# A two-layer attention trunk on one core: when the first rows are scaled, when two sets of weights are split, and which tiles the sine products use

## The chip, the cores and the metric

The kernel runs on one core of a Trainium2 chip. A core has five engines that work side by side, each on its own list of instructions: TensorE (PE, with its weight loads shown as PEld), VectorE (DVE), ScalarE (ACT), GpSimd (POOL) and SyncE (SP), which here only issues transfers (DMAs). An engine takes its instructions in order; where one waits, everything behind it on that engine waits too. The metric is the time of one execution in microseconds (us); the figure for a kernel is the median of its timed runs.

## The reference, cut to what matters

One sequence of 1024 tokens of width 1024 goes through two layers. All weights are float32. Before each of them the rows are normalised (RMS norm with a gain by column).

```python
def mla_swa_layer(x, ...):                         # layer 0
    z = rms_norm(x, g_in) @ w_in
    cq, ckv, kpe, q_s, k_s, v_s, gate = split_cols(z, EVEN_SPLITS)
    q  = rms_norm(cq, g_q_a) @ w_q_up              # 256 -> 8 heads of 64 + 32
    kv = rms_norm(ckv, g_kv_a) @ w_kv_up           # 128 -> 8 heads of 64 + 64
    # the 32 rotary columns of q and k are turned by the token's angle (cos, sin)
    o = concat(causal attention of q, kv; sliding window attention of q_s, k_s, v_s)
    return x + (o * silu(gate)) @ w_out
def fox_layer(x, ...):                             # layer 1
    q, k, v, f_logit, gate = split_cols(rms_norm(x, g_in) @ w_in, ODD_SPLITS)
    log_cum = cumsum(log_sigmoid(f_logit + b_f))   # bias log_cum[t] - log_cum[s] on the logits
    return x + (causal attention with that bias * silu(gate)) @ w_out
```

The output is the RMS norm of the last rows, times a gain.

## The kernel before, in words

**Number format.** Every operand of a product is held as two tiles, a high part (names with h: hh, wh, qh, kh) and the remainder (hl, wl, ql, kl). A product is three matmuls: L118 (high by high), L119, L120. The high part is a cast on ACT (L107 for rows, L112 and L792/L803 for weights), the low part is a subtraction: on DVE for rows (L108, which reads PSUM), on POOL for weights (L115, L805). A step of one input chunk or one weight tile is called its split.

**The start.** The token rows 0 to 511 lie in four tiles xrows[0..3] (called r in the profile), rows 512 to 1023 in xrows[4..7] (ld, kx). While they are loaded, PE runs 46 matmuls on zeros (L587, from tile ob). DVE and ACT sum the squares of rows 0 to 3 (L147, L150), DVE makes the inverse roots (`inv_rms`, twelve small instructions, L127 to L142). Then the rows are scaled, in two column halves (0 to 511, then 512 to 1023), each half in four instructions: row tile 0 on POOL (L287), row tile 1 on ACT (L795), row tiles 2 and 3 on DVE (L797). Between the halves a table of 19 gains is turned (PE L801) and copied (DVE L802, tile gains); every split of a chunk needs it. Behind them POOL makes the low parts of the four first weight tiles (L805) and a mask (L806).

**The first loop** (L812) goes over eight column chunks of 128, k = 0..7: PE turns the chunk's four 128x128 blocks (L216; here T0 to T7; T0 to T3 read the first column half, T4 to T7 the second), ACT makes hh (L107), DVE makes hl (L108), and one chunk later PE multiplies by the first weights (`latent_q`, L690, here L0 to L7: twelve matmuls each, first four with hh and the high weights, then four with hl, then four with the low weights). The turned blocks lie in PSUM tiles named s and t in turn, two of each. Between the chunks stand the sums of squares of rows 4 to 7 (k < 4), their `inv_rms` (k = 4) and scaling (k = 5, POOL L287 three times and DVE L824). For k > 5 two steps of `zb_steps` are taken in each turn: a step casts (ACT L112) and subtracts (POOL L115) one tile of the second weights, 288 columns wide, into kh and kl (six tiles) and kx (two tiles). These are used by `latent_kv`, eight chunks of three matmuls for each block of 128 tokens.

**Queries.** `up_q` (L914) multiplies the normalised latent by its weights; for the 32 rotary columns DVE multiplies the result by a table of cosines and by one of sines (L928), each into a tile of tag "r0", and SP stores the tile. Tag r0 has four buffers, tag "og" two.

**Values of layer 1.** Three groups of columns (256, 384, 384) are multiplied for all eight token blocks. `value_weights` loads and splits the weights of one group; those of group 2 (qh, ql, kh, kl) are asked for behind the last block of group 1. The forget logits come out of group 0; they are turned (PE L1281), summed along the sequence (lcs), stored and read back as the bias tiles ld.

**What sets the order.** In the start the code fixes the order of PE, DVE, ACT and POOL as it is written; later parts are put in order by a scheduler that follows the code's order and what is ready by its own estimate, so that moving a call moves its instructions on every engine.

Of the kernel before, what the change touches and what calls it, by code (L numbers as in the profile page):

```python
# [19 lines left out]
P = 128  # L20
S = 1024
D = 1024
NB = S // P
# [28 lines left out]
WORK0 = "q1 g0 q2 s0 q3 s1 s2 s3 a1 p0 b1 g2 p1 g3 p2"  # L52
WARM = 46
W_START0 = "FFFLLFLFLF"
# [7 lines left out]
def trunk(ctx, tc, x, positions, e_g_in, e_w_in, e_g_q_a, e_w_q_up, e_g_kv_a, e_w_kv_up,  # L62
          e_sinks, e_w_out, o_g_in, o_w_in, o_b_f, o_w_out, g_final, out):
    nc = tc.nc
    x, out = x[0], out[0]
# [29 lines left out]
    def pst(tag, n=512):  # L95
        count[0] += 1
        t = ps.tile([P, 512], F32, tag=tag, name=f"{tag}{count[0]}", bufs=BANKS[tag])
        return t[:, :n]
# [476 lines left out]
    gst = sbt("bs", [P])  # L575
# [9 lines left out]
    with tc.manual_schedule(engines={mybir.EngineType.PE}):  # L585
        for j in range(WARM):
            nc.tensor.matmul(out=idle, lhsT=zeros[:, 0:P], rhs=zeros[:, 0:512], start=True, stop=True)  # L587
# [188 lines left out]
    with tc.manual_schedule(engines={ET.PE, ET.DVE, ET.Activation, ET.Pool}):  # L776
# [8 lines left out]
        nc.vector.tensor_scalar(out=ssq[:, 3:4], in0=part[:, 0:1], scalar1=part[:, 1:2], scalar2=None, op0=ALU.add)  # L785
        y = inv_rms(ssq, 4, D)
        for k in range(0, KC, 4):
# [3 lines left out]
        for (wl, wh), raw in list(zip(za_low, za_raw))[:3]:  # L791
            nc.scalar.copy(out=wh, in_=raw)  # L792
        for c in (slice(0, 512), slice(512, D)):
            normalise(xrows[0][:, c], y[:, 0:1], 1.0)
            nc.scalar.activation(out=xrows[1][:, c], in_=xrows[1][:, c], func=AF.Copy, scale=y[:, 1:2])  # L795
            for b in (2, 3):
                nc.vector.tensor_scalar(out=xrows[b][:, c], in0=xrows[b][:, c], scalar1=y[:, b:b + 1],  # L797
                                        scalar2=None, op0=ALU.mult)
            if c.start == 0:
                g_ps = pst("pj", 32)  # L800
                nc.tensor.transpose(out=g_ps[:, 0:19], in_=gst[0:19], identity=ident[0:19, 0:19])  # L801
                nc.vector.tensor_copy(out=gains, in_=g_ps[:, 0:19])  # L802
        nc.scalar.copy(out=za_low[3][1], in_=za_raw[3])  # L803
# [7 lines left out]
        for k in range(KC + 2):  # L811
            made = next(turns, None) or made  # L812
            if k == 1:
                steps = latent_q(0)
            if k > 1:
                next(steps)
            if k < 4:
                square_sum(xrows[4 + k], ssq[:, k:k + 1], k == 1)
            if k == 4:
                y = inv_rms(ssq, 4, D)  # L820
            if k == 5:
                for b in range(3):
                    normalise(xrows[4 + b], y[:, b:b + 1], 1.0)
                nc.vector.tensor_scalar(out=xrows[7], in0=xrows[7], scalar1=y[:, 3:4], scalar2=None, op0=ALU.mult)  # L824
            if k > 5:
                for _ in range(2):
                    next(zb_steps, None)
# [86 lines left out]
    def up_q(g, i):  # L914

        for hf in range(2):
# [4 lines left out]
            if i < 2:  # L921
                st = sbt("r0", [512])
                nc.scalar.copy(out=st, in_=acc)
                nc.sync.dma_start(out=qns[2 * g + i, :, cols], in_=st)
            else:
                for table, to in ((cosT, qcs), (sinT, qss)):
                    st = sbt("r0", [512])
                    nc.vector.tensor_tensor(out=st, in0=acc, in1=table[:, cols], op=ALU.mult)  # L928
                    nc.sync.dma_start(out=to[g, :, cols], in_=st)
# [319 lines left out]
    for g in range(3):  # L1249
        c0, c1, parts, n = made  # L1250
        for blk in range(NB):
# [5 lines left out]
            if c0 == 0:  # L1257
                nc.vector.tensor_tensor(out=flog[:, blk, :], in0=acc[:, c1:n], in1=bf_b, op=ALU.add)
            if g < 2 and blk == (4 if g == 0 else NB - 1):
                made = value_weights(*groups[g + 1])  # L1260
# [195 lines left out]
```

## Time and profile before

| | us |
|---|---|
| timed runs | 1189.61, 1192.16, 1192.25 (median 1192.16) |
| the profiled execution | 1190.83 |
| its span, first to last instruction | 1189.0 |
| PE busy | 1161.2 (98%) |
| DVE, ACT, POOL busy | 716.0, 702.7, 588.8 (60%, 59%, 50%) |

The profiled execution is 1.8 us longer than its span and 1.3 us below the median. All positions below are us from the start of the span. In a row of the timeline the columns are start, duration, engine, line, operation, output tile <- input tiles, shape and count; in square brackets stands the idle time of the engine before it and what ended it. The matmuls overlap, so that the distance of two starts is what one costs.

### The profile page before, as it was taken

What the parts mean: (1) busy time and instruction counts of PE and PEld (TensorE: products, weight loads), DVE (VectorE), ACT (ScalarE), POOL (GpSimd) and SP (SyncE); (2) the same over time, 40 slices, a digit from 0 to 9 for tenths busy, and PEclk for the clock granted to TensorE, in tenths of its full rate; (3) what the DMA queues carried; (4) which work ended last, traced back from release to release, by engine and by line L of the source; (5) the groups of instructions that cost most, each with busy time, mean ns of one, the idle gap of its engine ahead of it and who ended that gap; (6) DMA issues with size and microseconds to landing.
All of it is one profiled execution on the core that took longest, in us unless ns stands there. A gap on an engine that the chain in (4) does not pass through costs nothing. (4 is left out here: it accounts for less than half of the span.)

```text
span 1189.0 us, 19541 instructions
## 1 busy us (share of the span) xinstructions
PE 1161.2 (98%) x6384; PEld 994.2 (84%) x6384; DVE 716.0 (60%) x1905; ACT 702.7 (59%) x1565; POOL 588.8 (50%) x717
## 2 busy tenths in 40 slices
PE   9999999999999999999999999999999999999997
PEld 6897788888888877899898888888888888887886
DVE  6672366687767766662103666665666666657754
ACT  6445567776666665554115766676767676766532
POOL 6411245474665453333404556656555555568452
PEclk9999999999999999999999999999999999999999
DMA  5327522453654442654322222313122223237441
GB/s 203 105 56 265 122 55 73 123 151 116 175 165 117 130 149 81 201 171 137 110 97 62 64 71 63 89 56 96 60 84 65 81 68 96 65 124 230 154 158 63
DMA packets 155357, 135.26 MB, mean 114 GB/s; under 512 B 53580, under 2 KB 119911, under 8 KB 155255
## 3 DMA queue, kind: packets, MB, share of 16 engines
q1 hardware_dynamic: 155254, 134.02, 38.1%
q8 instruction: 50, 0.82, 0.3%
q14 instruction: 53, 0.43, 0.1%
HBM read 96.43 MB, written 37.55 MB: 113 GB/s over the span
## 5 line engine op out<-in xcount | busy, mean ns | idle before, releaser
L118 PE MATMUL pj<-hh,wh 128*128 128x512 f32 (+1 forms) x792 | 320.4, 405 | 1.2 <-DVE ql L248 1.2
L120 PE MATMUL pj<-hh,wl 128*128 128x512 f32 (+1 forms) x792 | 308.9, 390 | 0.0
L119 PE MATMUL pj<-hl,wh 128*128 128x512 f32 (+1 forms) x792 | 308.8, 390 | 0.0
L115 POOL TENSOR_TENSOR wl<-wr,wh 128x512 fp32r<-128x512 f32 (+1 forms) x130 | 164.2, 1264 | 149.9 <-ACT wh L112 140.9
L105 DVE TENSOR_TENSOR pl<-t,ph 128x512 fp32r<-128x512 f32 (+1 forms) x320 | 179.0, 564 | 85.9 <-ACT ph L104 83.9
L287 POOL TENSOR_SCALAR r<-r,sm 128x256 f32<-128x256 f32 (+4 forms) x250 | 169.8, 688 | 123.1 <-DVE sm L334 66.6
L104 ACT CAST ph<-t 128x512 fp32r<-128x512 f32 (+1 forms) x320 | 153.9, 484 | 112.4 <-PE t L358 93.2
L120 PEld LDWEIGHTS pj<-hh,wl 128*128 128x128 f32 x792 | 148.8, 188 | 32.5
L332 ACT ACTIVATE r<-r,sm 128x128 f32<-128x128 f32 (+7 forms) x184 | 143.1, 778 | 54.1 <-DVE sm L325 52.5
L118 PEld LDWEIGHTS pj<-hh,wh 128*128 128x128 f32 x792 | 149.4, 189 | 22.8 <-issue 1.6
L119 PEld LDWEIGHTS pj<-hl,wh 128*128 128x128 f32 x792 | 149.7, 189 | 20.5
L358 PE MATMUL t<-ident,r 128*128 128x128 f32 x828 | 135.8, 273 | 7.9 <-DVE pl L105 5.1
L358 PEld LDWEIGHTS t<-ident,r 128*128 128x128 f32 x828 | 103.8, 140 | 35.8 <-DVE pl L105 6.3
L112 ACT CAST wh<-wr 128x512 fp32r<-128x512 f32 (+1 forms) x130 | 77.6, 598 | 60.0 <-PE pj L119 27.3
L319 POOL TENSOR_TENSOR ld<-ld,zrow 128x128 f32<-128x128 f32 x128 | 58.4, 465 | 105.8 <-DVE sm L325 79.2
L349 PE MATMUL o<-ph,v 128*128 128x512 f32 (+3 forms) x288 | 107.5, 373 | 0.0
L350 PE MATMUL o<-pl,v 128*128 128x512 f32 (+3 forms) x288 | 99.8, 347 | 0.0
L325 DVE CUSTOM_DVE_ANT_0 r<-s,ld 128x512 f32<-128x512 f32 (+1 forms) x120 | 67.6, 563 | 47.8 <-PE s L272 45.4
L296 POOL TENSOR_TENSOR v<-ge,v 128x512 fp32r<-128x512 f32 x26 | 33.8, 1300 | 68.7 <-ACT v L295 68.6
L349 PEld LDWEIGHTS o<-ph,v 128*128 128x128 f32 x288 | 54.7, 190 | 7.7
L350 PEld LDWEIGHTS o<-pl,v 128*128 128x128 f32 x288 | 54.9, 191 | 6.3
L248 DVE TENSOR_TENSOR qh<-pj,qh 64x512 fp32r<-64x512 f32 x24 | 16.4, 685 | 65.1 <-ACT qh L247 64.8
(335 smaller groups left out, 2355.6 us busy)
## 6 DMA issues: line engine op xcount, KB each, us to landing
wr<-in_o_w_in SPq DMA_DIRECT2D x50, 256.0 KB, 2.9
ld<-lcs SPq DMA_DIRECT2D x16, 512.0 KB, 4.3
ogs<-og SPq DMA_DIRECT2D x28, 256.0 KB, 2.0
wr<-ogs SPq DMA_DIRECT2D x28, 256.0 KB, 3.3
ge<-vscr SPq DMA_DIRECT2D x24, 256.0 KB, 3.9
gt<-x1s SPq DMA_DIRECT2D x23, 256.0 KB, 2.6
wr<-ogs SPq DMA_DIRECT2D x24, 192.0 KB, 2.9
wr<-in_e_w_in SPq DMA_DIRECT2D x16, 256.0 KB, 3.6
```

The costliest lines, as they stand in the source:

```text
L104: nc.scalar.copy(out=hi, in_=src)
L105: nc.vector.tensor_tensor(out=lo, in0=src, in1=hi.bitcast(F32), op=ALU.subtract)
L112: cast = nc.scalar.copy(out=hi, in_=raw)
L115: (engine or nc.gpsimd).tensor_tensor(out=lo, in0=raw, in1=hi.bitcast(F32), op=ALU.subtract)
L118: nc.tensor.matmul(out=o, lhsT=ah, rhs=bh, start=first, stop=False)
L119: nc.tensor.matmul(out=o, lhsT=ah, rhs=bl, start=False, stop=False)
L120: nc.tensor.matmul(out=o, lhsT=al, rhs=bh, start=False, stop=last)
L287: nc.gpsimd.tensor_scalar(out=row, in0=row, scalar1=rc, scalar2=scale, op0=ALU.mult, op1=ALU.mult)
L332: nc.scalar.activation(out=row[:, 0:L], in_=row[:, 0:L], func=AF.Exp, scale=-1.0, bias=mn, accum_out=den)
L349: nc.tensor.matmul(out=O[0][:, cols], lhsT=v()[:, j, :], rhs=ph[:, cols], start=j == 0, stop=False)
L350: nc.tensor.matmul(out=O[0][:, cols], lhsT=v()[:, j, :], rhs=pl[:, cols], start=False, stop=j == n - 1)
L358: nc.tensor.transpose(out=t[:, b * P:(b + 1) * P], in_=rows[b][:, j * P:(j + 1) * P], identity=ident)
```

## The change

1. The zero matmuls are cut from 46 to 45; 34 stand ahead of the turning of the gains and 11 behind it.
2. The scaling of the second column half of rows 0 to 3 is put into the loop at k = 1, behind the splits of chunks 0 and 1.
3. The steps of the second weights are taken from k = 3 on instead of k = 6.
4. The sine products of `up_q` go to tiles of tag "og".
5. The weights of the third value group are asked for behind block 4 of the second group, instead of its last block.

```diff
-WARM = 46
+WARM, WARM_FIRST = 45, 34
...
-        for j in range(WARM):
+        for j in range(WARM_FIRST):
             nc.tensor.matmul(out=idle, lhsT=zeros[:, 0:P], rhs=zeros[:, 0:512], start=True, stop=True)
...
-        for c in (slice(0, 512), slice(512, D)):
+        def scale_first(c):
             normalise(xrows[0][:, c], y[:, 0:1], 1.0)
             nc.scalar.activation(out=xrows[1][:, c], in_=xrows[1][:, c], func=AF.Copy, scale=y[:, 1:2])
             for b in (2, 3):
                 nc.vector.tensor_scalar(out=xrows[b][:, c], in0=xrows[b][:, c], scalar1=y[:, b:b + 1],
                                         scalar2=None, op0=ALU.mult)
-            if c.start == 0:
-                g_ps = pst("pj", 32)
-                nc.tensor.transpose(out=g_ps[:, 0:19], in_=gst[0:19], identity=ident[0:19, 0:19])
-                nc.vector.tensor_copy(out=gains, in_=g_ps[:, 0:19])
+
+        y = y_first
+        scale_first(slice(0, 512))
+        g_ps = pst("pj", 32)
+        nc.tensor.transpose(out=g_ps[:, 0:19], in_=gst[0:19], identity=ident[0:19, 0:19])
+        for j in range(WARM - WARM_FIRST):
+            nc.tensor.matmul(out=idle, lhsT=zeros[:, 0:P], rhs=zeros[:, 0:512], start=True, stop=True)
+        nc.vector.tensor_copy(out=gains, in_=g_ps[:, 0:19])
...
             if k == 1:
+                scale_first(slice(512, D))
                 steps = latent_q(0)
...
-            if k > 5:
+            if k > 2:
                 for _ in range(2):
                     next(zb_steps, None)
...
-                for table, to in ((cosT, qcs), (sinT, qss)):
-                    st = sbt("r0", [512])
+                for table, to, tag in ((cosT, qcs, "r0"), (sinT, qss, "og")):
+                    st = sbt(tag, [512])
...
-            if g < 2 and blk == (4 if g == 0 else NB - 1):
+            if g < 2 and blk == 4:
                 made = value_weights(*groups[g + 1])
```

In the lists that follow a row is line, operation, output <- inputs and shape; tiles carry their number. Lines behind 583 stand up to five lines lower in the changed kernel.

**DVE at the start, before**, from the scaling of the first column half (L797, tiles r) through the splits of chunks 0 to 2 (L108) and a sum of squares of row tile 5 (L147):

```order
L797 TENSOR_SCALAR r_75<-r_75,sm_229 128x512
L802 COPY gains<-pj_254 128x19
L797 TENSOR_SCALAR r_73<-r_73,sm_229 128x512
L797 TENSOR_SCALAR r_75<-r_75,sm_229 128x512
L108 SCALAR_TENSOR_TENSOR hl_271<-s_272,gains,hh_270 128x512
L108 SCALAR_TENSOR_TENSOR hl_271<-t_281,gains,hh_270 128x512
L147 ISA ge_288,sm_269<-ld_176 128x1024
```

The same place in the changed kernel:

```order
L797 TENSOR_SCALAR r_75<-r_75,sm_217 128x512
L806 COPY gains<-pj_242 128x19
L108 SCALAR_TENSOR_TENSOR hl_266<-s_267,gains,hh_265 128x512
L108 SCALAR_TENSOR_TENSOR hl_266<-t_276,gains,hh_265 128x512
L797 TENSOR_SCALAR r_73<-r_73,sm_217 128x512
L797 TENSOR_SCALAR r_75<-r_75,sm_217 128x512
L147 ISA ge_287,sm_264<-ld_164 128x1024
```

The two scalings of the second column half have changed places with the first two splits.

**POOL at the start, before**: the scaling of row tile 0 (L287, two halves in one row), the low parts of the first weights (L805), the mask (L806), three tiles made from it (L1024), the scaling of row tiles 4 to 6 (ld, kx) and the first of eight low parts of the second weights (kl):

```order
L287 TENSOR_SCALAR r_69<-r_69,sm_229 128x512 x2
L805 TENSOR_TENSOR ql_244<-wr_166,qh_243 128x512
...
L806 AFFINE_SELECT d_191<-d_191 128x256
L1024 TENSOR_SCALAR bs_1643<-d_191 128x256
...
L287 TENSOR_SCALAR ld_174<-ld_174,sm_357 128x1024
L287 TENSOR_SCALAR ld_176<-ld_176,sm_357 128x1024
L287 TENSOR_SCALAR kx_178<-kx_178,sm_357 128x1024
L115 TENSOR_TENSOR kl_414<-wr_415,kh_413 128x288
```

and in the changed kernel:

```order
L287 TENSOR_SCALAR r_69<-r_69,sm_217 128x512
L809 TENSOR_TENSOR ql_232<-wr_154,qh_231 128x512
...
L810 AFFINE_SELECT d_179<-d_179 128x256
L287 TENSOR_SCALAR r_69<-r_69,sm_217 128x512
L1029 TENSOR_SCALAR bs_1642<-d_179 128x256
...
L115 TENSOR_TENSOR kl_336<-wr_337,kh_335 128x288
L115 TENSOR_TENSOR kl_336<-wr_342,kh_335 128x288
L115 TENSOR_TENSOR kl_336<-wr_382,kh_335 128x288
L115 TENSOR_TENSOR kl_388<-wr_389,kh_387 128x288
L287 TENSOR_SCALAR ld_162<-ld_162,sm_368 128x1024
```

The second half of row tile 0 now stands behind the four low parts and the mask, and four low parts of the second weights stand ahead of the scaling of row tiles 4 to 6; the casts for them stand on ACT between the splits of chunks 4 to 7, two to a chunk.

**POOL at the end of the second value group, before**: clearing four tiles (L256) for layer 1's keys, and the low parts of the last three of the third group's qh tiles:

```order
L256 MEMSET kx_7560 64x1024
L256 MEMSET kx_7561 64x1024
L256 MEMSET kx_7856 64x1024
L256 MEMSET kx_7857 64x1024
L115 TENSOR_TENSOR ql_7172<-wr_7173,qh_7171 128x384
L115 TENSOR_TENSOR ql_7182<-wr_7183,qh_7181 128x384
L115 TENSOR_TENSOR ql_7182<-wr_7187,qh_7181 128x384
```

and in the changed kernel:

```order
L115 TENSOR_TENSOR ql_7087<-wr_7088,qh_7086 128x384
L115 TENSOR_TENSOR ql_7097<-wr_7098,qh_7096 128x384
L115 TENSOR_TENSOR ql_7097<-wr_7102,qh_7096 128x384
L256 MEMSET kx_7559 64x1024
L256 MEMSET kx_7560 64x1024
L256 MEMSET kx_7855 64x1024
L256 MEMSET kx_7856 64x1024
```

The low parts have moved ahead of the clearing; their casts on ACT stand behind the fifth copy of the second group instead of the eighth. On PE the eight turnings of the forget logits (L1281; three stood inside the second group, five behind it) all stand behind the last value product now, and with them the sum lcs, its store and the reading back of its first bias tiles.

## Rows read from the trace of the kernel before

**Rows 1.** The page: busy us (share) and number of instructions, PE.

```profile
PE 1161.2 (98%) x6384; PEld 994.2 (84%) x6384; DVE 716.0 (60%) x1905; ACT 702.7 (59%) x1565; POOL 588.8 (50%) x717
```

**Rows 2.** Waits of PE: line <- what released it: us in total, times, longest.

```profile
PE t L358 <- DVE pl L105: 5.1, 3, 1.9
...
PE pj L119 <- POOL ql L115: 1.1, 2, 0.6
...
PE pj L118 <- ACT kx L112: 0.8, 1, 0.8
...
PE pj L119 <- POOL kx L115: 0.5, 1, 0.5
PE pj L118 <- ACT qh L112: 0.5, 1, 0.5
```

**Rows 3.** Timeline of PE at the start: low products of L0, T4, of L2.

```profile
17.38 0.50 PE L690 MATMUL pj<-qh,hl 128*128 128x256 f32 x2 [1.28 <-DVE hl L108]
...
20.31 0.60 PE L216 MATMUL s<-ident,r 128*128 128x128 f32 x4
...
21.22 0.40 PE L690 MATMUL pj<-qh,hl 128*128 128x256 f32 x2
```

**Rows 4.** Timeline of DVE at the start.

```profile
4.61 1.23 DVE L147 CUSTOM_DVE_ANT_0 ge<-r 128x1024 bf16<-128x1024 f32 x1 [1.98 <-DMA r<-in_x]
...
14.13 2.54 DVE L797 TENSOR_SCALAR r<-r,sm 128x512 f32<-128x512 f32 x2
16.59 0.74 DVE L108 SCALAR_TENSOR_TENSOR hl<-s,gains,hh 128x512 fp32r<-128x512 f32 x1
...
17.91 2.22 DVE L147 CUSTOM_DVE_ANT_0 ge<-ld 128x1024 bf16<-128x1024 f32 x1
...
22.34 0.16 DVE L127 TENSOR_SCALAR sm<-sm 128x4 f32<-128x4 f32 x1
```

**Rows 5.** Timeline of POOL at the start.

```profile
11.90 1.81 POOL L287 TENSOR_SCALAR r<-r,sm 128x512 f32<-128x512 f32 x2 [8.12 <-DVE sm L142]
13.69 5.36 POOL L805 TENSOR_TENSOR ql<-wr,qh 128x512 fp32r<-128x512 f32 x4
19.00 1.39 POOL L806 TENSOR_SCALAR_AFFINE_SELECT d<-d 128x256 f32<-128x256 f32 x1
...
24.63 2.67 POOL L287 TENSOR_SCALAR ld<-ld,sm 128x1024 f32<-128x1024 f32 x2 [2.77 <-issue]
...
28.39 3.84 POOL L115 TENSOR_TENSOR kl<-wr,kh 128x288 fp32r<-128x288 f32 x5
```

**Rows 6.** Timeline of PE in the first block of `latent_kv`, and what follows it.

```profile
32.42 0.29 PE L120 MATMUL pj<-kh,hl 128*128 128x288 f32 x1
...
34.41 0.29 PE L120 MATMUL pj<-kh,hl 128*128 128x288 f32 x1
...
37.49 0.38 PE L216 MATMUL s<-ident,ld 128*128 128x128 f32 x2
```

**Rows 7.** Timeline in `up_q`: DVE's cosine and sine products, PE's next product.

```profile
112.68 0.69 DVE L928 TENSOR_TENSOR r<-pj,r 128x512 f32<-128x512 f32 x1 [0.40 <-DMA kts<-r]
114.18 0.69 DVE L928 TENSOR_TENSOR r<-pj,r 128x512 f32<-128x512 f32 x1 [0.81 <-DMA qcs<-r]
...
114.93 0.50 PE L118 MATMUL pj<-qh,ph 128*128 128x512 f32 x1 [0.94 <-DVE r L928]
```

**Rows 8.** Timeline of POOL and PE around the third value group.

```profile
582.39 4.01 POOL L256 MEMSET kx<- 64x1024 f32 x4 [9.28 <-PE pj L120]
...
585.23 0.71 PE L1281 MATMUL t<-ident,gt 128*16 128x128 f32 x5
...
620.80 0.33 PE L118 MATMUL pj<-kh,hh 128*128 128x384 f32 x1
...
621.84 0.39 PE L118 MATMUL pj<-hh,wh 128*128 128x512 f32 x1
```

**Rows 9.** Stretches of PE: from:to, length, busy (instructions), granted clock, DMA share, GB/s.

```profile
426.00:430.00 4.00, 3.89 (x12) 0.57 0.88 271
```

More of the change, by code (lines that the diff above doesn't have):

```diff
@@ L785, in trunk @@
         nc.vector.tensor_scalar(out=ssq[:, 3:4], in0=part[:, 0:1], scalar1=part[:, 1:2], scalar2=None, op0=ALU.add)
-        y = inv_rms(ssq, 4, D)
+        y_first = inv_rms(ssq, 4, D)
         for k in range(0, KC, 4):
```

## The prediction

> **What bounds the kernel now.** I read the page's busy shares first. PE is busy for 1161.2 us of a span of 1189.0, 98% [rows 1], and no other engine passes 60%. So the time is PE's work plus some 28 us in which it stands, and an edit that takes no work from PE can win only what it takes out of those 28 us. The list of PE's waits came next, since it tells what ended each of them; the ones that the change can touch are few [rows 2]. The largest waits there (for the attention's pl tiles, 5.1 us in three) lie in stretches whose instructions stand in the same order as before. Then I read the timeline at the four places that the edits touch: the start, the first block of the second projection, the rotary queries, and the third value group. In each the reader is to look for two things: how long PE stood, and which engine's queue held the tile that it waited for.
>
> **The start (edits 1 and 2).** PE stands for 1.28 us ahead of the low products of L0, which begin at 17.38 [rows 3]. It waits for hl of chunk 0, and that split began only at 16.59, behind 2.54 us of scaling of the second column half [rows 4]. With the scaling moved behind the splits, hl 0 begins when hh 0 is made, at about 15.1 to 15.3 (0.7 for the cast behind T0), and ends about 0.74 later [rows 4], at about 15.9 to 16.0, when PE is just done with its high products. So the wait of 1.28 is gone, and the zero matmul that is left out brings T0 forward by about 0.2. Nothing is gained by that at once, since T4 reads the second half, and who scales it last is now late. On POOL the second half of row tile 0 stands behind four low parts (5.36 us) and the mask (1.39 at most). One half takes 1.81 / 2 = 0.9 [rows 5], so: first half done at 12.8, low parts at 18.2, mask at 18.6 to 19.5, second half at 19.5 to 20.4. T4 stood at 20.31 [rows 3], and without the wait it could start at about 18.9; it starts at about 19.6, so half of the gain is used up there. DVE takes the rest. Its queue is now hl 0, hl 1, the two scalings, the sum of squares, hl 2: 16.7 at the end of hl 1, plus 1.3 to 2.5 for the scalings, plus 1.3 to 2.3 for the sum with its read-out, plus 0.74. That gives hl 2 at 20.0 to 22.2; I take 21.45, since POOL's low parts and mask still run beside the scalings and the later part of the sum runs free. The low products of L2, which began at 21.22 [rows 3], begin then at about 21.5. So 1.28 us of stall at L0 comes back as a shorter one at T4 and one of about a microsecond at L2: **+0.3 us, bounds -0.5 to +1.0**. From L2 on the chunks follow each other at PE's pace.
>
> The two price ends of this term come from rows. The same sum of squares takes 1.23 us at 4.61 and 2.22 at 17.91 [rows 4], when POOL makes low parts and the mask [rows 5]. DVE and POOL hold each other up here; the splits from PSUM are not touched (0.74 in the midst of POOL's low parts [rows 4]).
>
> The Trainium skill has a rule for that, "SBUF — State Buffer", section "Who interferes with whom": GpSimd and a VectorE instruction in a two-port mode, or with two SBUF inputs, share one pair of ports, and whichever starts first holds it for its whole instruction. The rows on L147 agree (2.22 against 1.23). By that rule this change would do something more, which is the first rival below.
>
> **The second weights (edit 3).** The first block of the second projection uses kh and kl without a wait, and then stands for the kx tiles: 0.8 us for the cast, 0.5 for the low part [rows 2]. The whole loss is read from the starts: 15 matmuls from 32.42 to 34.41, so 0.133 each; from 34.41 to the next instruction at 37.49 there are seven, which takes 0.93, and it took 3.08 [rows 6]. **2.15 us are lost.** In the changed order all eight casts stand between the splits of chunks 4 to 7, and POOL makes four low parts ahead of the scaling of rows 4 to 6 and four behind. A low part takes 3.84 / 5 = 0.77 [rows 5], so POOL has 4 x 0.77 ahead, 2.67 / 2 = 1.3 for each of three row tiles [rows 5], 4 x 0.77 behind: from about 22 to 32. The kx tiles are needed at 34.5. The cover is some 2 us wide, and I take the whole loss as gone: **-2.15, bounds -2.2 to -1.4** (the last low part late by 0.8, one POOL instruction). What it adds is two casts on ACT in each of four turns, an engine that is busy for 59% of the span [rows 1], and the risk that a cast which waits for its weights holds the next hh; later waits in this stretch move along with PE.
>
> Behind the weights stands DVE's `inv_rms`: twelve instructions of 0.16 from 22.34 on [rows 4], now beside POOL's first four low parts. Ahead POOL was idle then. If each is held up by the neighbour, they end up to 2.5 us later, and with them hl 5 and hl 6; PE would stand for up to about 1.0 of that. I put **+0.55 (0 to +1.1)** for it, half way, since the rows on L147 show a loss of 0.99 in 2.22 us, which is not a full stop. The start in sum: 0.3 - 2.15 + 0.55 = **-1.3, bounds -2.7 to +0.7**.
>
> **The sine products (edit 4).** A cosine and a sine product each wait for a buffer: 0.40 for the store of keys, 0.81 for the store of an earlier cosine product [rows 7]. PE's next matmul needs the bank that the sine product reads, so it starts at 114.93 after a wait of 0.94 [rows 7]. With a tile of the other tag the second sine product needs no store; tag og holds nothing there whose store is still under way. The cosine product then starts 0.4 earlier, since the r0 buffers turn over at half the pace, and the sine one directly behind: 112.3 + 2 x 0.69 = 113.7, ahead of PE's last matmul there. The wait of 0.94 goes, with the refill of about 0.15 that comes with it: **-1.1, bounds -1.25 to 0** (nothing, if another store is late in its place). Nothing is added; two tiles change place.
>
> **The third value group (edit 5).** It goes from 585.23 to 621.84 [rows 8], 36.61 us. It has 8 x 24 = 192 matmuls; six starts from 620.80 to 621.84 give 0.1735 each [rows 8], so 33.3, and the five turnings cost about 0.6. **2.7 us are lost**, 0.5 of it at the cast and 1.1 at the low parts in the list [rows 2], the rest in shorter stands behind them. The low parts are late because POOL clears four tiles from 582.39 for 4.01 us first [rows 8], and the casts because ACT's copy of the last block stands ahead. In the new order casts and low parts follow the fifth copy, some 12 us before they are needed, and clearing comes after. All of it goes, but for the usual small stands: **-2.4, bounds -2.7 to -1.0**. The eight turnings and their sum move behind the products; the work is the same, so PE loses nothing there, but the bias lcs and the loads behind it in SP's queue come some 30 us later, and POOL's and PE's first key products follow closely. I find about 0 to 0.55 us of cover missing for one cast behind the load ge, and 0.4 to spare for the low part next to it; that is the near end of the bound.
>
> **Sum.** -1.3 - 1.1 - 2.4 = -4.8 us on an execution of 1190.8: 1186.0. The median of the runs stands 1.3 above that execution, so the same gain gives 1187.3 against it; I take the middle, **1186.7**. The bounds added up (-6.6 to -0.3) are too wide for independent terms; from the two runs' bases I take 1184.3 to 1189.0 for this case.
>
> **The rivals.**
>
> *The start gives nothing.* By the skill's rule above each of the twelve `inv_rms` instructions with two SBUF inputs would wait for a whole low part of POOL. As a mechanism of this kernel: hl 5 and hl 6 late by 2.5 us, stands at L5 and L6 of 1 to 1.5, hl 2 at 22.2, the mask at its long price. The start is then +1.0 + 1.5 - 2.15 = +0.3, the sum -3.2 and the time 1187.6 to 1189.0, say 1188.6. For it: L147 at twice its price beside POOL [rows 4]. Against: PE needs only hl from DVE, and hl 5 to 7 have room while L2 to L4 run.
>
> *The value group keeps half.* The late lcs chain takes the place of the old wait: its loads stand ahead of the loads for the first key product's weights, and PE waits there for 1 to 1.5 us. Sum -3.5, time 1188.0. For it: the load is issued behind the stores of the last block. Against: the first key product has some 0.4 us of cover in my count, and the bias itself is needed 20 us later.
>
> *The sine wait is replaced.* Another store of a tile r0 is late, since the DMA queue is the same: sum -3.7, 1187.7.
>
> *Slower: the clock falls in the first loop.* Once in this trace PE stood for 1.9 us [rows 2], and in the 4 us behind that the granted clock was 0.57, half way to the lower level [rows 9], which cost about 4 x 0.43 = 1.7 us. At T4 to L6 PE will stand at two or three places, where before it stood at one. If two of them pass 1.9 us, with weights that land late and hold ACT's casts ahead of hh 6 and hh 7, the loop loses 2 x 1.7 for the clock and 3 to 4 for the stands: start +5 instead of -1.3, time about 1193 to 1195. Against it: no stand of 1.3 us at the start lowered the clock, and the longest that I find there is about 1 us. It decides from two stands of 1.9 us on.
>
> **How the numbers follow.** The forecast 0.58; the start gives nothing 0.17; the value group keeps half 0.12; the sine wait replaced 0.06; slower 0.07. A measurement of this kernel can tell about 0.3%, 3.6 us, from no change, so faster means below 1188.6 and slower above 1195.7. The forecast lies below 1188.6 nine times in ten (0.52), the first rival half of the time (0.08), the next two in about half (0.09): faster 0.69; slower 0.02 to 0.03 of the last rival; the rest within. The range reaches to 1190.8, where the start and the value group both give little and the base is the median.
>
> **What would show it.** In the changed profile hl 0 ends before 16.2 and PE's wait of 1.28 is gone, with a stand of about 1 us ahead of L2's low products and one of about 0.5 at T4; the first block of `latent_kv` ends at about 35.5 to 36.5, with no wait for kx; no wait for L928's successor at 113.9; no wait for qh or ql behind the second value group; clock 1.00 in the first 40 us. Wrong would be stands of more than 1.5 us at L5 to L7, a granted clock below 1 there, or a new wait of PE at the first key product of layer 1 of over 1 us.

## The result, and the profile after

The changed kernel took 1184.54 us (median of three; 1183.48 to 1184.86) where the kernel before took 1192.16: a ratio of 0.9945, 95% interval 0.9928 to 0.9962. So it is faster, by 7.6 us between the medians and by 4.5 to 8.6 us by the interval. Measured twice more beside the experiments it came to 0.9935 (0.9921 to 0.9949) and 0.9959 (0.9943 to 0.9975). The prediction said 1186.7, range 1184.3 to 1190.8; the median lies 0.2 us inside its lower end. The profiled execution took 1183.48 us with a span of 1181.7, against 1190.83 and 1189.0.

PE's busy time fell by 3.7 us, from 1161.2 [rows 1] to this row of the page after. Its work is the same but for a single zero matmul, so something besides its stands had become shorter:

```profile
PE 1157.5 (98%) x6383; PEld 992.8 (84%) x6383; DVE 715.8 (61%) x1905; ACT 702.9 (59%) x1565; POOL 586.3 (50%) x717
```

The list of PE's waits after (line <- what released it: us in total, times, longest). Of the waits of [rows 2], those for kx, qh and POOL's ql are gone, and a new one for POOL's scaled row r stands second:

```profile
PE t L358 <- DVE pl L105: 5.1, 3, 1.9
PE s L216 <- POOL r L287: 2.1, 1, 2.1
...
PE pj L118 <- DVE ql L248: 0.6, 1, 0.6
```

To see where the time went I set the start of each matmul in one trace against the same matmul in the other. The distance of the two is constant while both run alike, and steps where one of them waits:

| stretch (us, before) | step of PE against before | what it is |
|---|---|---|
| up to T0 | -0.65 | T0 at 13.28 instead of 13.93 |
| T0 to the end of the first loop | +1.5 | T4 waits for POOL |
| second projection, first block | -2.15 | no wait for kx |
| 38 to 110 | -0.2 | at 64, wait for a row of L698 0.6 instead of 0.8 |
| rotary queries, 113 to 115 | -1.15 | no wait for a buffer |
| 133 | -0.7 | wait for ql 0.6 instead of 1.2 |
| 426 to 430 | -1.3 | the clock did not fall |
| third value group | -2.7 | no waits for qh, ql |
| whole span | -7.3 | |

**Start.** Timeline of PE after: T0, the low products of L0, T4, the low products of L2, the first kx product, and the next block's first turning. L0's wait of 1.28 [rows 3] is gone, T4 waits for 2.09 instead, L2 for nothing, and kx follows without a gap:

```profile
13.28 0.60 PE L216 MATMUL s<-ident,r 128*128 128x128 f32 x4
...
15.45 0.50 PE L690 MATMUL pj<-qh,hl 128*128 128x256 f32 x2
...
20.62 0.65 PE L216 MATMUL s<-ident,r 128*128 128x128 f32 x4 [2.09 <-POOL r L287]
...
21.59 0.40 PE L690 MATMUL pj<-qh,hl 128*128 128x256 f32 x2
...
35.39 0.29 PE L118 MATMUL pj<-kx,hh 128*128 128x288 f32 x1
...
36.19 0.38 PE L216 MATMUL s<-ident,ld 128*128 128x128 f32 x2
```

DVE and POOL after, in the same stretch. DVE's two scalings now stand behind hl 1, the sum of squares (L147) follows them, and the first of the twelve `inv_rms` instructions takes 0.77 where it took 0.16 [rows 4]. POOL's second half of row tile 0 takes 1.90, where two halves took 1.81 together [rows 5]:

```profile
16.93 2.03 DVE L797 TENSOR_SCALAR r<-r,sm 128x512 f32<-128x512 f32 x2
18.88 1.21 DVE L147 CUSTOM_DVE_ANT_0 ge<-ld 128x1024 bf16<-128x1024 f32 x1
...
22.70 0.77 DVE L127 TENSOR_SCALAR sm<-sm 128x4 f32<-128x4 f32 x1
...
26.48 0.75 DVE L108 SCALAR_TENSOR_TENSOR hl<-t,gains,hh 128x512 fp32r<-128x512 f32 x1
```

```profile
18.66 1.90 POOL L287 TENSOR_SCALAR r<-r,sm 128x512 f32<-128x512 f32 x1
20.54 1.37 POOL L1029 TENSOR_SCALAR bs<-d 128x256 f32<-128x256 f32 x3
21.87 3.10 POOL L115 TENSOR_TENSOR kl<-wr,kh 128x288 fp32r<-128x288 f32 x4
```

**Rotary queries.** DVE after: cosine and sine product directly behind each other, no idle time in brackets where [rows 7] has 0.40 and 0.81. PE's next product starts 0.23 behind the one ahead of it:

```profile
110.89 0.69 DVE L933 TENSOR_TENSOR r<-pj,r 128x512 f32<-128x512 f32 x1
111.50 0.68 DVE L933 TENSOR_TENSOR og<-pj,r 128x512 f32<-128x512 f32 x1
```

```profile
112.13 0.39 PE L120 MATMUL pj<-qh,pl 128*128 128x512 f32 x1
112.36 0.39 PE L118 MATMUL pj<-qh,ph 128*128 128x512 f32 x1
```

**Third value group.** POOL and PE after: the low parts are made at 569, before the clearing and 11 us before their use; the group begins at 580.69 and PE's next work at 613.97, 33.3 us for 192 matmuls. Behind the eight turnings the next product follows, and from there to 660 PE's timeline has no idle time in brackets in this execution (the experiments show others in which it has):

```profile
569.42 2.96 POOL L115 TENSOR_TENSOR ql<-wr,qh 128x384 fp32r<-128x384 f32 x3 [0.46 <-ACT qh L112]
577.86 4.00 POOL L256 MEMSET kx<- 64x1024 f32 x4 [5.48 <-PE pj L120]
```

```profile
580.69 0.33 PE L118 MATMUL pj<-qh,hh 128*128 128x384 f32 x1
...
613.97 0.71 PE L1286 MATMUL t<-ident,gt 128*16 128x128 f32 x5
614.44 0.48 PE L118 MATMUL pj<-hh,wh 128*128 128x512 f32 x1
```

**Clock.** The wait ahead of the place of [rows 9] is there after, as long as before (1.86 against 1.85), and yet the granted clock stays at 1.00 (columns as in [rows 9]):

```profile
422.83 0.79 PE L358 MATMUL t<-ident,r 128*128 128x128 f32 x3 [1.86 <-DVE pl L105]
```

```profile
424.00:428.00 4.00, 4.00 (x27) 1.00 0.91 271
```

Those 4 us are 1.3 us of the gain in this pair of executions. Whether they belong to the change had to be tested.

### The profile page after: what moved, and what is told of

Its sections match the earlier page's. It is cut to its first block, busy times and chain, and to the rows that moved or that the text cites. A ratio compares the mean times of both kernels' runs of the same rounds, so it can differ in the third digit from the quotient of the medians.

```text
span 1181.7 us, 19530 instructions
## 1 busy us (share of the span) xinstructions
PE 1157.5 (98%) x6383; PEld 992.8 (84%) x6383; DVE 715.8 (61%) x1905; ACT 702.9 (59%) x1565; POOL 586.3 (50%) x717
## 5 line engine op out<-in xcount | busy, mean ns | idle before, releaser
L287 POOL TENSOR_SCALAR r<-r,sm 128x256 f32<-128x256 f32 (+4 forms) x250 | 169.9, 687 | 122.3 <-DVE sm L334 65.3
L119 PEld LDWEIGHTS pj<-hl,wh 128*128 128x128 f32 x792 | 149.5, 189 | 20.5
L319 POOL TENSOR_TENSOR ld<-ld,zrow 128x128 f32<-128x128 f32 x128 | 58.2, 464 | 99.7 <-DVE sm L325 78.8
L279 DVE TENSOR_TENSOR og<-o,ob 64x512 f32<-64x512 f32 x64 | 43.9, 686 | 11.2 <-ACT ob L278 10.1
```

Of the source, the lines that this page charges most:

```text
L119: nc.tensor.matmul(out=o, lhsT=ah, rhs=bl, start=False, stop=False)
L287: nc.gpsimd.tensor_scalar(out=row, in0=row, scalar1=rc, scalar2=scale, op0=ALU.mult, op1=ALU.mult)
```

## The experiments

The theory: every edit gives what stands in its own stretch of the table, and the rest (T0, the wait at 133, the clock) varies from execution to execution. The rival: the edits keep the clock up, or help each other. There were twelve runs. Times are medians; "before" is the kernel before, timed beside them.

**Single edits.** e1_start has edits 1 to 3 alone, e2_og edit 4 alone, e3_values edit 5 alone, each with the lines of the diff above and no others; e0_after is the changed kernel.

> The kernel before with edits 1 to 3 (the start) alone; sine products and value weights as before. Theory (each edit gives what stands in its own stretch of the two traces, and the rest of the 7.3 us is the clock behind 424 us): PE reaches the second block of the second projection about 1.3 us earlier than before, with a wait of about 2.1 us at T4, and the time falls by 1.2 to 1.5 us, 0.1%. If PE's clock does not fall near 424 in this run, 1.3 us more. Rival (the edits help each other; the start sets off the later gains): 3 us or more, with a shorter stand in the rotary queries or at the third value group.

> The kernel before with edit 4 alone (sine products in tiles og). Theory: 1.1 us at the rotary queries and another 0.6 to 0.7 at the wait for ql at about 134 us, which shrinks from 1.2 to 0.6, since the stores that the next loads wait for go out earlier: 1.7 to 1.9 us in all, 0.15%, and 1.3 more where the clock does not fall near 424. Rival (the shorter wait at 134 comes from the start or from chance): 1.1 us, and the wait at 134 is 1.2 again.

> The kernel before with edit 5 alone (third value weights behind block 4). Theory: the third group loses its waits for qh and ql, 2.7 us, nothing is given back at the first key product: 2.5 to 2.8 us, 0.22%, and 1.3 more where the clock does not fall near 424. Rival (the late chain of the forget logits costs something when the rest stands as before): 1.2 to 2.0 us, with a new wait of PE between 620 and 660.

> The changed kernel once more, beside the single edits on the same chip. Theory: 6.0 us from the edits (1.3, 1.8, 2.7 and small ones), and 1.3 more in executions in which the clock stays up behind the wait of 1.86 us at about 421; so the mean granted clock of the executions goes with their time, here as in the kernel before. Rival (the change keeps the clock up): clock 0.999 in all executions of this kernel, 0.996 in all of the kernel before, and a gain of 7.3 us throughout.

| kernel | executions | median us | ratio to before (95%) | mean clock |
|---|---|---|---|---|
| before | 17 | 1193.84 | | 0.996 |
| e1_start | 11 | 1191.66 | 0.9981 (0.9969 to 0.9992) | 0.996 |
| e2_og | 6 | 1189.01 | 0.9963 (0.9950 to 0.9976) | 0.997 |
| e3_values | 5 | 1188.77 | 0.9961 (0.9949 to 0.9973) | 0.997 |
| e0_after | 6 | 1185.88 | 0.9935 (0.9921 to 0.9949) | 0.998 |

Each edit alone is faster, e1_start by the least (its interval ends at 0.9992). In the traces each gives its own step and no other edit's: -1.2 at the rotary queries in e2_og, -2.7 at the third value group in e3_values, no wait for kx in e1_start. The medians add up to more than that, 4.8 and 5.1 us for the two later edits, because the executions differ by up to 5 us and their clocks with them. The rival that the changed kernel holds 0.999 throughout is out: its executions show 0.995 to 0.999, and the slowest, 1188.96 us, has 0.995. That time goes with the clock is right.

Where the clock fell differed between the profiles: near 426 before, 338 in e3_values, 424 in e2_og, nowhere in e0_after, and twice in e1_start, behind T4 and near 426. At T4 the wait was 2.25 us, and the matmuls behind it stand 0.43 apart, where 0.24 is usual:

```profile
20.70 0.92 PE L216 MATMUL s<-ident,r 128*128 128x128 f32 x4 [2.25 <-POOL r L287]
...
22.27 0.63 PE L690 MATMUL pj<-qh,hl 128*128 128x256 f32 x2
22.70 0.63 PE L690 MATMUL o<-qh,hl 128*128 128x256 f32 x2
```

The rival of e3_values, that the late chain of the forget logits costs something, came half true. From the first product behind the third group to one 25 us later, the five profiles without edit 5 all take the same time (to 0.01 us). The nine with edit 5 take 0.1 to 1.3 us more, 0.55 in the mean: 0.1 in the first profile after, 0.6 in e3_values, 1.0 in e0_after, 1.3 in e7_row0_early (below). In that last one PE waits for the low part of a weight tile (wl) of layer 1's first keys and queries. POOL makes it behind the bias tiles (L319), and these wait for their load from lcs. In the kernel before the first L319 was long done, at 598.70, some 20 us ahead of that product. PE and POOL in e7_row0_early, then POOL before:

```profile
631.89 0.50 PE L120 MATMUL pj<-hh,wl 128*128 128x512 f32 x1 [0.81 <-POOL wl L115]
```

```profile
629.73 0.88 POOL L319 TENSOR_TENSOR ld<-ld,zrow 128x128 f32<-128x128 f32 x2 [2.17 <-DMA ld<-lcs]
630.57 1.27 POOL L115 TENSOR_TENSOR wl<-wr,wh 128x512 fp32r<-128x512 f32 x1
```

```profile
598.70 0.88 POOL L319 TENSOR_TENSOR ld<-ld,zrow 128x128 f32<-128x128 f32 x2 [6.84 <-DMA ld<-lcs]
```

**The start taken apart.** e5_scale is e1_start with the second weights from k = 6 again:

```diff
-            if k > 2:
+            if k > 5:
                 for _ in range(2):
                     next(zb_steps, None)
```

> The kernel before with edits 1 and 2 alone (second column half scaled behind two splits; second weights from k = 6 as before). Theory (these two edits only move the stand from L0 to T4): no wait at L0, a wait of about 2.1 at T4, as in the changed kernel, because POOL's second half of row tile 0 takes 1.9 us beside DVE's sum of squares instead of 0.95; the twelve instructions of inv_rms take 2.0 us again instead of 3.8, because POOL is idle then; L7 ends 0.3 us later than in the kernel before, measured from T0; the stand at kx is 2.1 as before. Time within 0.5 us of the kernel before, and 1.3 more where the clock falls behind T4. Rival (the scaling gives the gain of 1.3, the weights nothing): 1.0 us or more faster, with no stand at kx.

One execution, 1192.51 us, which by itself tells nothing beside executions of before from 1188.6 to 1196.8; the trace does. The wait at T4 is 2.25, the stands at kx are back, and POOL's scaling takes 1.65. The twelve instructions are quick again, since POOL is idle then; the first starts at 22.96 and the last ends at 25.1, and hl 5 waits for ACT and no more for DVE's own queue:

```profile
19.08 1.65 POOL L287 TENSOR_SCALAR r<-r,sm 128x512 f32<-128x512 f32 x1
```

```profile
22.96 0.16 DVE L127 TENSOR_SCALAR sm<-sm 128x4 f32<-128x4 f32 x1
...
25.62 0.75 DVE L108 SCALAR_TENSOR_TENSOR hl<-t,gains,hh 128x512 fp32r<-128x512 f32 x1 [0.52 <-ACT hh L107]
```

The expectation was wrong in one number: the loop ends not 0.3 us later than before, but 2.8 (19.3 us from T0 to the last product of L7 against 16.5). T4 itself is 1.2 later, and the 1.6 behind it is the clock, which fell there here too: from T4 to the last product of L7 it is 11.7 us against 10.1. Edits 1 and 2 by themselves cost time; all that the start wins is the second weights.

**What T4 waits for.** e6_sq_act is the changed kernel with the sum of squares of row tile 5 on ACT:

```diff
-                square_sum(xrows[4 + k], ssq[:, k:k + 1], k == 1)
+                square_sum(xrows[4 + k], ssq[:, k:k + 1])
```

> The changed kernel with the sum of squares of row tile 5 on ACT instead of DVE. Theory (DVE and POOL hold each other up; the sum of 1.2 us is what POOL's last scaling waits for): that scaling takes 0.95 instead of 1.90, T4 starts at about 19.7 instead of 20.6, PE's wait there is about 1.1 instead of 2.1, and PE reaches the second projection 0.5 to 0.9 us earlier. Rival (the scaling is slow by itself at that place, or T4 waits for another row): 1.9 us and a wait of 2.1 again.

1187.78 us, one execution. The scaling takes 0.85 and T4 starts 0.97 earlier: it was the sum on DVE that held POOL. But PE stands 0.81 us for hl at L5 later, so that the second block comes 22.74 us behind T0 instead of 22.91. Of 0.97 us 0.17 is left; the 0.5 to 0.9 that I expected there is not.

```profile
18.74 0.85 POOL L287 TENSOR_SCALAR r<-r,sm 128x512 f32<-128x512 f32 x1
```

```profile
19.65 0.66 PE L216 MATMUL s<-ident,r 128*128 128x128 f32 x4 [1.03 <-POOL r L287]
27.20 0.50 PE L690 MATMUL pj<-qh,hl 128*128 128x256 f32 x2 [0.81 <-DVE hl L108]
```

**Three attempts at a better version.** e7_row0_early scales POOL's second half between the second and the third low part:

```diff
-        for (wl, wh), raw in zip(za_low, za_raw):
+        for i, ((wl, wh), raw) in enumerate(zip(za_low, za_raw)):
+            if i == 2:
+                normalise(xrows[0][:, 512:D], y[:, 0:1], 1.0)
             nc.gpsimd.tensor_tensor(out=wl, in0=raw, in1=wh.bitcast(F32), op=ALU.subtract)
...
         def scale_first(c):
-            normalise(xrows[0][:, c], y[:, 0:1], 1.0)
+            if c.start == 0:
+                normalise(xrows[0][:, c], y[:, 0:1], 1.0)
```

> The changed kernel with POOL's second half of row tile 0 between the second and third low part of the first weights. Theory (POOL's place in the queue sets T4): T4 starts at about 19.0, when DVE's scalings end, so its wait shrinks from 2.1 to 0.7; the sum of squares on DVE now meets the last low part and the mask and takes up to 2.2, so that hl of chunk 2 comes at 20.7 to 22 and the low products of L2 begin at 20.9 to 22.0 (21.6 in the changed kernel). Time 0 to 0.7 us below the changed kernel, and no fall of the clock behind T4 in any execution. Rival (T4 is late for another reason): wait 2.1 again.

e8_row0_sq adds the exchange of the sums (`k == 2` for `k == 1` in the line on square_sum):

> As the last one, and the sum of squares that DVE makes is that of row tile 6 behind the split of chunk 2 (ACT makes that of row tile 5 in its place). Theory: T4 at about 19.0, hl of chunk 2 at 19.7, no wait ahead of the low products of L2, which begin at about 20.0: PE 1.3 to 1.6 us ahead of the changed kernel at L2, and 0.8 to 1.5 us below it in time, if the weights for the second projection keep up. Rival (ACT, which then has the sum ahead of hh of chunk 2, or POOL's low parts of the weights, which L4 needs, become the bound): PE stands at L3 to L5 instead and the time is that of the changed kernel.

e9_inv_rms adds that the second `inv_rms` stands at k = 5 instead of 4 and the scaling of rows 4 to 7 at k = 6 instead of 5:

> As the last kernel (row tile 0 early, sum of squares of row tile 6 on DVE), and the twelve small instructions of the second inv_rms stand behind the split of chunk 5 instead of ahead of it, the scaling of rows 4 to 7 one chunk later. Theory (DVE's queue is what gives the gain back: hl of chunk 5 stands behind instructions that wait for POOL's low parts, so PE stands 1.2 us at L5): no wait of PE at L5, the loop ends 1.0 to 1.2 us earlier than in the kernel with the two other edits, PE at the second block of the second projection about 21.5 us behind T0 (22.6 there, 22.9 in the changed kernel), and 1.0 to 1.4 us off the time of the changed kernel. Rival (rows 4 to 7 become late, or the casts that wait for weights on ACT hold hh of chunk 6): the wait moves to L6 or to the turning of rows 4 to 7, and the time is that of the changed kernel.

| kernel | executions | median us | ratio to before (95%) | second block behind T0, us |
|---|---|---|---|---|
| changed kernel | | | | 22.91 |
| e7_row0_early | 7 | 1187.74 | 0.9958 (0.9939 to 0.9978) | 22.90 |
| e8_row0_sq | 6 | 1187.01 | 0.9945 (0.9924 to 0.9965) | 22.62 |
| e9_inv_rms | 6 | 1187.08 | 0.9955 (0.9940 to 0.9969) | 23.01 |

None is shown to beat the changed kernel. In each the wait at T4 shrinks as expected and comes back one step on. In e7_row0_early T4 waits 0.64, and L2 waits 1.21 for hl of chunk 2, behind the scalings (2.54 beside POOL) and the sum:

```profile
19.52 0.33 PE L216 MATMUL s<-ident,r 128*128 128x128 f32 x1 [0.64 <-DVE r L798]
21.53 0.51 PE L690 MATMUL pj<-qh,hl 128*128 128x256 f32 x2 [1.21 <-DVE hl L108]
```

In e8_row0_sq L2's low products begin at 20.02, 1.57 earlier than in the changed kernel, and PE then waits 1.18 at L5. The reason is in DVE's queue: hl 5 stands behind the twelve instructions, and those of them that meet POOL's low parts of the second weights take 0.73 instead of 0.16:

```profile
27.07 0.50 PE L690 MATMUL pj<-qh,hl 128*128 128x256 f32 x2 [1.18 <-DVE hl L108]
```

```profile
24.25 0.73 DVE L141 TENSOR_TENSOR sm<-sm,sm 128x4 f32<-128x4 f32 x1
...
26.27 0.75 DVE L108 SCALAR_TENSOR_TENSOR hl<-t,gains,hh 128x512 fp32r<-128x512 f32 x1
```

In e9_inv_rms hl 5 stands ahead of them and the wait is at L6, 1.27 us, for hl 6, which now stands behind them; they meet six low parts and take 4.4 us in all, from 23.74 to 28.17. The rival of that expectation came true (the wait is at L6), though for another reason than it named:

```profile
28.89 0.51 PE L690 MATMUL pj<-qh,hl 128*128 128x256 f32 x2 [1.27 <-DVE hl L108]
```

```profile
26.05 0.74 DVE L141 TENSOR_TENSOR sm<-sm,sm 128x4 f32<-128x4 f32 x1
...
28.09 0.74 DVE L108 SCALAR_TENSOR_TENSOR hl<-s,gains,hh 128x512 fp32r<-128x512 f32 x1
```

**What belongs to the change and what to the execution.** e10_og_values has edits 4 and 5 without the start, e0b_after is the changed kernel once more, e11_before is the kernel before, for a second profile.

> The kernel before with edits 4 and 5 and the start as before. Theory (the two later edits give their own 1.1 and 2.7 us, the start about 0.4 more): 3.8 us at an equal granted clock. Rival (the total of some 6.4 us at an equal clock is made by something that the start adds in most executions, and that the profile of before, one of its faster executions, does not show): the same 3.8 us, and then the start is worth some 2.5 us. Third possibility (the later edits take away waits for transfers that vary from execution to execution and that this one profile shows too small): 5 to 6 us.

> The changed kernel a third time, beside the last two. Theory: 1184 to 1189 us, time going with the granted clock at about 0.76 us for each 0.001; the stand at T4 is 2.0 to 2.3 us and lowers the clock behind it in some executions and not in others.

> The kernel before once more, for a second profile of it. Theory (T0, the waits for transfers and the places where the clock falls vary from execution to execution): T0 begins between 13.1 and 13.9 us, the wait for ql at about 134 us is anywhere from 0.5 to 1.5, the clock falls somewhere else than near 426 or nowhere, and the waits at L0, kx, L928 and qh, ql are there again. Rival (what differs between the two first profiles belongs to the change): 13.9, 1.2 and a fall near 426 again.

e11_before took 1188.99 us and settles the three odd rows of the first table. T0 begins at 13.24, earlier than in the changed kernel's first profile; PE's wait for ql near 133 is 1.5; L0 waits 1.02. PE stands for 1.9 us around 424 (it is busy for 3.62 and 2.50 us of two stretches of 4), the longest wait for pl in the list is 2.3, and the clock stays at 1.00 here and everywhere behind T0, where it was 0.57 in [rows 9]:

```profile
PE t L358 <- DVE pl L105: 5.6, 3, 2.3
...
PE pj L118 <- DVE ql L248: 1.5, 1, 1.5
```

```profile
16.43 0.50 PE L690 MATMUL pj<-qh,hl 128*128 128x256 f32 x2 [1.02 <-DVE hl L108]
```

```profile
420.00:424.00 4.00, 3.62 (x20) 1.00 0.20 70
424.00:428.00 4.00, 2.50 (x12) 1.00 0.82 249
```

So the kernel before has executions with these 1.3 us and without them. The wait for ql was 0.5 to 1.5 in nine profiles with edit 4 (mean 0.9) and 0.7 to 1.5 in five without it (mean 1.2): it is mostly the execution's, so what e2_og was expected to show there is no effect of the edit that these profiles could tell; one of 0.3 us stays possible.

e0b_after took 1187.35 us (1185.40 to 1189.99, six executions, one of them above the expected 1189; before 1192.72, 17 executions). T4 waits 2.26 there and the clock falls behind it, in the changed kernel itself:

```profile
22.00:26.00 4.00, 4.00 (x24) 0.62 0.40 96
```

e10_og_values took 1187.40 us, ratio 0.9971 (0.9956 to 0.9986), so 3.5 us, between 1.7 and 5.2, while the medians lie 5.3 apart. The 3.8 of the theory fits, and the 5 to 6 of the third possibility lies at the end of the interval. What parts the theory from its rival is what the start adds, 0.4 or 2.5 us; at an equal clock (below) the changed kernel stands 1.2 us, standard error 0.5, under e10_og_values, between the two, and so that stays open. Its clock fell at 36 us, where the waits for kx stand, which only edit 3 removes:

```profile
34.00:36.00 2.00, 1.01 (x4) 1.00 0.66 192
36.00:38.00 2.00, 1.91 (x9) 0.55 0.65 193
```

To put the medians on one footing I took all 114 executions of the nine kernels that were timed repeatedly, and fitted one straight line of time against mean granted clock with a level of its own for each kernel. The slope is 0.84 us (standard error 0.09) for each 0.001 of mean clock. At equal clock the kernels stand against the one before at: e1_start -1.5, e2_og -2.4, e3_values -2.9, e10_og_values -4.4, changed kernel -5.6 (standard errors 0.4 to 0.65); e7_row0_early, e8_row0_sq and e9_inv_rms stand 0.2, 0.8 and 0.5 above the changed kernel (0.65 each). The mean clock of the changed kernel's 15 executions was 0.9976, that of before's 46 was 0.9964, which by the slope is 1.0 us more. Together that is 6.6 of the 7.0 us by which the medians of all executions differ (1193.0 and 1186.0).

The steps in the traces add up to less than the 5.6: 0.4 for the start from T0 on, 1.15 for the sine products, and 2.7 less 0.55 for the value weights, so some 3.7. Part of the reason can be read: the two profiled executions of the kernel before lie 2.4 and 2.6 us under its own line in the fit, the three of the changed kernel 0.4 to 1.7. So both traces of before are from executions that were short for their clock, and what the longer ones lose stands in no trace. Some 1.9 us of the gain at equal clock therefore have no stretch of their own.

## Why the prediction was right

The sum was -4.8 us; at equal clock it is -5.6 with a standard error of 0.4, and against the second profile of before the span is 5.5 shorter (4.2 with e0_after's span of 1183.0). The mechanisms of edits 3, 4 and 5 are the predicted ones, but that the number comes so near is in part luck. The first pair's -7.3 holds 2.65 us that no edit made (T0, the wait at 133, the clock); the steps that the edits do make come to 3.7 where the sum had 4.8; and 1.9 of the 5.6 are not placed. Point by point:

- **The sine products, -1.1.** Right: -1.15 in the first pair, -1.2 in e2_og, by the mechanism that was named. DVE's products follow each other [rows 7 against the rows after].
- **The value weights, -2.4 of a loss of 2.7.** Right in mechanism, and all 2.7 went inside the group. The rival that the late chain of the forget logits costs half of it came true in part: PE loses 0.1 to 1.3 us behind the group in the nine profiles with edit 5 and nothing in the five without. That leaves -2.2 in the mean. The prediction had the place (the first key product) and put the missing cover at 0 to 0.55.
- **The second weights, -2.15.** Right to 0.05: the stretch from the last product of L7 to the second block took 7.05 before (30.44 to 37.49) and takes 4.90 (31.29 to 36.19).
- **T0, the moved scaling and `inv_rms`, +0.3 and +0.55, bounds -0.5 to +2.1 together.** The sum for the start, -1.3, was met in the first pair (37.49 to 36.19), but not by these steps. From T0 to the second block it is 23.3 in e11_before, e2_og and e3_values and 22.9 in the changed kernel: -0.4. The other 0.9 is the one profile that I had: T0 began at 13.93 there, and at 13.0 to 13.5 in all others, with this start and with that, and L0 waited 1.28 instead of 1.02. That the zero matmul left out brings T0 forward by 0.2 is not shown by them. From T0 to the last product of L7 the changed kernel takes 18.0, the start of before takes 16.0 to 16.5; so moving the scaling and the slower `inv_rms` cost +1.5 to +2.0 together, where I had +1.05 from T0 on (+0.85 with T0's 0.2 in it).
- **The step that was mis-sized** is POOL's second half of row tile 0. I took 0.9 us for it from [rows 5]; it took 1.90 beside DVE's sum of squares, and 0.85 without (e6_sq_act). I had given DVE's instructions a price beside POOL and POOL's none beside DVE. With 1.90 the half ends at 20.5, which is where T4 starts: 7.3 us behind T0 instead of 5.9 to 6.4, so +1.0 to +1.5 for moving the scaling, where I had +0.5 from T0 on. On the other side the sum on DVE took 1.21 and no more, hl 2 was there at 20.8, and L2 did not wait, where I had expected a stand of about 1 us.
- **The first rival** (the twelve instructions wait for POOL's low parts) came half true. They took 3.8 us instead of 2.0, by whole stops of 0.7, not the partial loss that I argued from L147; in the changed kernel T4's late start hides all but 0.5 of it (counted from T4, L5's low products begin 0.1 later than before and L6's 0.3 more). So the +0.55 was right in size, though I had reached it by halving. Here the rule of the Trainium skill, "SBUF — State Buffer", section "Who interferes with whom", describes the rows better than my reading did: whoever starts first holds the shared ports for its whole instruction, and the other stops. The 0.72 to 0.77 for an instruction of 0.16 agree with it (a low part takes 0.77). On POOL's side 1.90 against 0.85 shows a stop too, but POOL's row starts at 18.66, 0.2 us ahead of the sum's, and still it was POOL that stood; which of the two had come first the rows do not tell.
- **The slower rival** (the clock falls behind T4) does happen, in e1_start, e5_scale and e0b_after, behind waits of 2.25 and 2.26; a granted clock below 1 there was one of the prediction's signs of being wrong. It is in three of the five profiles with this wait and in none of the five with the start of before, so it comes with the change. It costs 1.0 us by the second block, and 1.6 in e5_scale, not the 5 of the rival: it falls once and not twice, and the casts of weights hold nobody. The rival's price for one fall, 1.7 us, was a little high; the fall of [rows 9] cost 1.3. Its reading of 0.57 as half way to the lower level is wrong: that level is 0.50 (e1_start from 22 to 24 us), so PE ran at it for most of those 4 us.

What the sum left out is the clock. I counted no gain from it; in the mean it gave 1.0 us. That the change lowers the number of falls, by taking away stands (kx, qh, ql) behind which it can fall, is argued from e10_og_values's rows at 36 us and not shown: e7_row0_early, with shorter stands at the start than the changed kernel (0.64 and 1.21 for 2.09) and none at kx, qh and ql, had a mean clock of 0.9959 in seven executions, below that of before.

## What to carry to other kernels

Before a profile's wait is booked as gain or loss, look for a second execution of the same kernel: here T0, one wait of 0.5 to 1.5 us and the place where the clock fell were the execution's and not the kernel's, together more than half of the predicted gain. When an instruction is moved beside work of the engine that it disturbs, price both sides, also the one whose row in the old trace was undisturbed. And follow a removed wait to the instruction that comes last next: around the start a microsecond won at T4 was for the most part waited for again at L2, L5 or L6 in four versions, because DVE's queue there was full. When a chain of loads is moved back, look in several executions at what stands behind it in the same queues.

## What the runs showed of the hardware

The granted clock fell to its lower level, half of the upper one, at places that changed between executions of one kernel. The wait near 424 is 1.85 or 1.86 us in all fourteen profiles: behind it the clock fell in five (before, e1_start, e2_og, e6_sq_act, e9_inv_rms) and stayed in nine. Near 337 it stayed behind 2.3 in e11_before and fell behind 2.8 in e3_values; at T4 it fell behind 2.25 and 2.26 (three profiles) and not behind 2.00 and 2.09 (two). A fall cost PE 1.2 to 1.6 us of its pace. Where a wait stands close behind, part of that is had back: in e7_row0_early the fall near 1088 swallowed a wait of 1.0 us that all other profiles but e9_inv_rms have there, and 0.3 us was left. Over 114 executions 0.001 of mean clock went with 0.84 us; that line takes up about half of the variance between executions of one kernel, whose spread is some 5 us.

A DVE instruction of 0.16 us took up to 0.84, mostly 0.71 to 0.77, where it met one of POOL's low parts, and a POOL scaling of 0.85 us took 1.65 to 1.90 beside a DVE sum of 1.2 to 1.4.
